# Mixture-of-experts stage of a two-block transformer: experts 0 and 1 placed ahead of the sort, 26 units of slots in place of 28

## The chip, the cores and the metric

One NeuronCore of a Trainium2 chip runs the whole program. The metric is the device time of one execution in microseconds (us); lower is better. The kernel before took 1778.32 us (median of 3 runs, 1778.24 to 1785.11).

## What is computed

A first transformer block (neighbourhood attention, grouped attention and a product-key expert layer) is followed by a second block (a gated-delta and an HGRN2 mixer, then a mixture of experts) and a last norm, on 256 tokens of width 1024 in fp32. The change lies in the mixture of experts alone:

```python
scores = sigmoid(xt @ w_router); sel = scores + router_bias
...
_, eidx = lax.top_k(where(emask, sel, -inf), TOP_K)      # 8 of 64 experts for each token
gates = ...                                              # normalised scores times 2.5
hg = einsum('td,edf->tef', x_b, w_gate)                  # every expert: 1024 -> 256, twice
hu = einsum('td,edf->tef', x_b, w_up)
routed = einsum('tef,efd->td', silu(hg) * hu * g, w_down)
shared = (silu(xt @ ws_gate) * (xt @ ws_up)) @ ws_down
```

With 256 tokens and 8 experts for each there are 2048 pairs of token and expert. The routing of the reference on these inputs leaves 14 experts with no token; the other 50 hold between 1 and 107.

## The kernel before

**Sort.** Once the router's scores are known, VectorE (DVE) picks each token's experts, counts the tokens of each expert, and ranks the 64 experts by falling count (`key`, `perm`). `lst` holds the expert of each rank as an address, `pos` and `V` hold for each token its place within the expert and its gate, both in the order of ranks. The counts and ranks are known only at the end of this chain; until then no weight of a routed expert can be addressed.

**Units.** The work on routed experts is cut into units of 128 slots (rows of TensorE's output). The 16 largest experts (`HEAVY`) have a unit of their own, ranks 16 to 29 share one in pairs of 64 slots, ranks 30 to 49 in fours of 32: 16 + 7 + 5 = 28 units, interleaved by a fractional key at the end of `moe`. If any expert has more tokens than its slots, or a rank past 49 has any, a branch at the end runs further units (`e.overflow`).

For each unit: `select` builds a 0/1 matrix S from `pos` (DVE), `tables` makes the slots' token numbers and gates from it (TensorE `pv`, DVE `sv` and `St`), `gather` multiplies the tokens by S, in 8 steps for a group of two units (TensorE `pga`, ScalarE `xg`), `gu_unit` multiplies by gate and up weights (`pgu`, 4 blocks of 128x1024 for each expert), `swiglu` and `turn` follow (`hh`, `phT`, `th`), `dn_block` multiplies by the down weights (`py`, 2 blocks for each expert), and `combine` adds the unit's rows back to the 256 tokens in two parts `yh` and `yl` (its output tiles show as `py` at L1771). An expert that has 64 or 32 slots uses 64 or 32 columns of the array: its matmul has that many stationary columns, and the experts of a unit lie side by side.

**Weights.** `wide_load` gives out buffers of 512 KB in a fixed ring (`load.raw`), and issues each load on the SP queue in program order. At this stage the ring has 25 places: 13 (11 of them `raw` tiles, 2 `mod` rows named `ada`), then 8 and 4 that held split weights (`whi`, `wlo`), which `load.raw.extend` adds just before `run`. A load waits until the last reader of its place is done. Before each load of a routed expert SP reads the expert's address from `lst` (`values_load`).

**Order.** The engines SP, PE, DVE and ACT run in the order in which the program is written (`m.manual`). In `run`, unit u goes through its four gate/up blocks, with steps of the next group's gather in between, then unit u - 2 is combined, then unit u - 1 goes through its down blocks. Two pieces of the shared expert (`shared_down`) stand within the sort.

Of the kernel before, what the change touches and what calls it, by code (L numbers as in the profile page):

```python
# [1393 lines left out]
HEAVY = 16  # L1394
MID = 30
LIGHT = 50
# [6 lines left out]
def wide_load(e, raw, parts):  # L1403
# [19 lines left out]
    return load  # L1423


def moe(e, a, x, m, late, out):
# [86 lines left out]
    def gu_unit(pg, xx, b, ws):  # L1513
        n = P // len(ws)
# [20 lines left out]
    def dn_block(py, th, k, w, last=True):  # L1535
        for q in range(2):
            for i in range(len(w)):
                t = slice(i * P // len(w), (i + 1) * P // len(w))
                nc.tensor.matmul(py[q][t], th[:, k, t], w[i][:, q * 512:(q + 1) * 512], start=k == 0, stop=last and k == 1)  # L1539
# [41 lines left out]
    wd = [load(a["ws_dn"][k], True) for k in range(2)]  # L1581
    hsh, psh = [], []

    def shared_down(tt, k):
        if k == 0:
            psh.append([ps.tile([P, 512], F32, tag="mm", name=uid(e, "py"), bufs=e.mm_bufs) for _ in range(2)])
        dn_block(psh[tt], hsh[tt], k, [wd[k]], last=False)
# [57 lines left out]
    nc.vector.scalar_tensor_tensor(num, pp[:, :2], 1.0, mk, op0=OP.add, op1=OP.mult)  # L1645
    idn = e.ident[:NE, :NE]
# [18 lines left out]
    more = pool.tile([1, 5], F32, name="more")  # L1665
    for k, (r, n) in enumerate(((0, 128.0), (HEAVY, 64.0), (MID, 32.0), (LIGHT, 0.0))):
        nc.vector.tensor_scalar(more[:, k:k + 1], pl[:, 1, r:r + 1], -n, 0.0, op0=OP.add, op1=OP.max)
    nc.vector.tensor_reduce(more[:, 4:5], more[:, 0:4], axis=AX.X, op=OP.max)
    moreu = pool.tile([1, 5], U32, name="moreu")
    nc.vector.tensor_copy(moreu, more)  # L1670
    pt = ps.tile([NE, 2, 2, P], F32, tag="tr", name="pT", bufs=e.tr_bufs)
# [3 lines left out]
    shared_down(1, 0)  # L1675
    tT = pool.tile([NE, 2, 2, P], F32, name="tT")
# [5 lines left out]
    shared_down(1, 1)  # L1682
    pos = pool.tile([P, 2, NE], F32, name="pos")
# [7 lines left out]
    def run(units, acc=()):  # L1691
# [10 lines left out]
        order = []  # L1702
        for u in range(len(units) + 1):
            for (which, n, v) in ((0, 4, u), (1, 2, u - 1)):
                if 0 <= v < len(units):
                    order += [(which, k, r) for k in range(n) for r in units[v][0]]
        ready = []
# [16 lines left out]
        def select(us):  # L1724

            S = wk.tile([P, 2, 2, P], F32R, tag="S", name=uid(e, "S"), bufs=2)
            for u, (ranks, base) in enumerate(us):
                r, n = ranks[0], len(ranks)
                nc.vector.tensor_tensor(S[:, :, u].rearrange("p t (r s) -> p t r s", r=n),
                                        io1[:, None, None, base:base + P // n].to_broadcast([P, 2, n, P // n]),  # L1730
                                        pos[:, :, r:r + n, None].to_broadcast([P, 2, n, P // n]), op=OP.is_equal)
            return us, S

        def tables(us, S):

            St = wk.tile([P, 2, T], F32R, tag="St", name=uid(e, "St"), bufs=4)
            sv = wk.tile([P, 2, 2], F32, tag="sv", name=uid(e, "sv"), bufs=3)
            pv = ps.tile([P, 2, 2], F32, tag="att", name=uid(e, "pv"), bufs=e.att_bufs)
            for u, (ranks, base) in enumerate(us):
                w = P // len(ranks)  # L1740
                for tt in range(2):
                    for i, r in enumerate(ranks):
                        t = slice(i * w, (i + 1) * w)
                        nc.tensor.matmul(pv[t, u], S[:, tt, u, t].bitcast(F32), V[:, tt, r], start=tt == 0, stop=tt == 1)
            n = len(us)
            nc.vector.tensor_copy(sv[:, :n], pv[:, :n])
            for u in range(n):
                nc.vector.tensor_scalar(St[:, u], iot, sv[:, u, 0:1], None, op0=OP.is_equal)
            xg = pool.tile([P, NC8, 2, P], F32, tag="xg", name=uid(e, "xg"), bufs=2)
            return S, St, [sv[:, u, 1:2] for u in range(n)], xg, us  # L1750

        def gather(g, q):

            S, xg, us = g[0], g[3], g[4]
            n = len(us)
            p = ps.tile([P, 2, P], F32, tag="att", name=uid(e, "pga"), bufs=e.att_bufs)
            steps = [(i, tt) for i in range(2) for tt in range(2)]
            for i, tt in steps:
                nc.tensor.matmul(p[:, :n].rearrange("p u n -> p (u n)"), hs[i][:, tt, q * P:(q + 1) * P],  # L1759
                                 S[:, tt, :n].rearrange("p u n -> p (u n)"), start=(i, tt) == steps[0],  # L1760
                                 stop=(i, tt) == steps[-1])
            nc.scalar.activation(xg[:, q, :n], p[:, :n], AF.Copy)  # L1762

# [10 lines left out]
        new, new2 = tables(*select(groups[0])), None  # L1774
        ahead(1)
        for q in range(2):
            gather(new, q)
        if len(groups) > 1:
            new2 = tables(*select(groups[1]))
# [3 lines left out]
        for u in range(len(units) + 1):  # L1783
            todo = []
            gi, i = divmod(u, 2)
            if u < len(units):
                if i == 0:
                    cur, new = new, new2
                if u == 0:
                    todo = [(cur, q) for q in range(2, 8)]  # L1790
                elif gi + 1 < len(groups):
                    todo = [(new, q) for q in range(4 if u > 1 else 0, 8)] if i else [(new, q) for q in range(4)]
                n, xx = len(units[u][0]), cur[3][:, :, i]
# [8 lines left out]
            for b in range(4):  # L1802
                if u < len(units):
                    gu_unit(pg, xx, b, weights(n))
                if b == 1 and h is not None:
                    th = turn(h)
                fetch(2 if u < 2 else FETCH[b])
# [13 lines left out]
            if done is not None:  # L1821
                py = down()
                n = len(units[u - 1][0])
                for k in range(2):
                    dn_block(py, th, k, weights(n))
# [31 lines left out]
    def shared_by(n, lo, hi, base):  # L1857
        return [(tuple(range(r, r + n)), base) for r in range(lo, hi, n)]


    kinds = [shared_by(1, 0, HEAVY, 0), shared_by(2, HEAVY, MID, 0), shared_by(4, MID, LIGHT, 0)]
    order = sorted(((j + (0.4, 0.6, 0.7)[k]) / len(us), u) for k, us in enumerate(kinds) for j, u in enumerate(us))
    units = [u for _, u in order]

    load.raw.extend([(early, 4, t) for _ in range(4) for t in ("whi", "wlo")])
# [112 lines left out]
```

## Time and profile before

| | |
|---|---|
| median of 3 runs | 1778.32 us (1778.24 to 1785.11) |
| the profiled execution | 1785.74 us, its span 1783.9 us |
| granted TensorE clock, mean over the span | 0.982 |
| busy: PE, DVE, ACT, POOL | 1687.5, 1133.2, 757.0, 192.8 us |
| the chain that ended last: PE, DVE, DMA | 68%, 17%, 7% of the span |
| bytes moved by DMA | 390.86 MB, mean 219 GB/s |
| weights of routed experts | 300 loads of 512 KB, issued from 1334.05 us on |

The span is the time from the first to the last instruction; what lies around it is 1.84 us here. In the 40 slices of the page each slice is 44.6 us; the mixture of experts takes the last ten. A matmul whose operands are fp32 appears twice in a view, as two records, so that one block of one expert's unit (two matmuls of 512 columns) is x4.

### The profile page before, as it was taken

The numbers are of one execution on the slowest core, as the hardware profiler recorded it, in microseconds if no ns is written. First come the engines' busy times: TensorE is split into PE (matmuls) and PEld (weight loads), VectorE is DVE, ScalarE is ACT, GpSimd is POOL, SyncE is SP. The second block draws the span as 40 slices with busy tenths as digits, with TensorE's granted clock in tenths as the row PEclk, the third lists the DMA queues.
The fourth block names the chain that finished last, engine by engine and source line by source line (L and its number), as shares of the span: only waits on it lengthen the run. The fifth ranks groups of instructions, "written<-read, shape, count | busy, mean of one in ns | idle before, by whom it ended". The sixth has DMA issues, their size and how long they took to land.

```text
span 1783.9 us, 28898 instructions
## 1 busy us (share of the span) xinstructions
PE 1687.5 (95%) x10939; PEld 1338.7 (75%) x10939; DVE 1133.2 (64%) x2209; ACT 757.0 (42%) x1240; POOL 192.8 (11%) x95
## 2 busy tenths in 40 slices
PE   6989998999999999999899998989989999999996
PEld 6778898999989999887678776978765554555543
DVE  5675789995979999777778676798571111111112
ACT  3557545344544444544444455655442222222222
POOL 1030001232112212000000003032020000000000
PEclk9999999999999999999999999999999999999998
DMA  6323654555435555688888754421129999999993
GB/s 232 128 83 118 210 161 152 159 173 189 154 125 163 172 170 166 200 285 292 280 282 285 246 182 149 159 95 48 76 91 409 409 395 362 375 364 340 410 356 122
DMA packets 108116, 390.86 MB, mean 219 GB/s; under 512 B 12657, under 2 KB 12945, under 8 KB 107841
## 3 DMA queue, kind: packets, MB, share of 16 engines
q1 hardware_dynamic: 106128, 384.58, 61.0%
q0 software_dynamic: 976, 2.82, 0.6%
q8 instruction: 88, 1.44, 0.3%
q10 hardware_dynamic: 864, 1.53, 0.3%
q14 instruction: 60, 0.48, 0.1%
HBM read 386.79 MB, written 2.10 MB: 218 GB/s over the span
## 4 chain that ended last, share of the span: by engine, by line
PE 68%; DVE 17%; DMA 7%; issue 4%; ACT 3%; POOL 0%; DVEq 0%; SPq 0%; ACTq 0%
PE pgu L1519 11%; PE acc L686 8%; DMA raw<-in_w_ada 6%; PE py L1539 6%; PE pu L80 5%; PE pu L82 5%; PE pu L81 5%; DVE wlo L67 5%; PE pga L1759 3%; PE py L1771 3%; PE pg L632 2%; ACT whi L66 2%; PE pmv L81 1%; PE pmv L82 1%; PE pmv L80 1%
## 5 line engine op out<-in xcount | busy, mean ns | idle before, releaser
L66 ACT ACTIVATE whi<-raw 128x1024 fp32r<-128x1024 f32 x366 | 384.5, 1054 | 306.3 <-PE pu L81 136.5
L67 DVE TENSOR_TENSOR wlo<-raw,whi 128x1024 fp32r<-128x1024 f32 x310 | 383.4, 1239 | 81.9 <-ACT whi L66 81.0
L82 PE MATMUL pu<-pxT,wlo 128*128 128x256 f32 x1024 | 289.6, 283 | 9.4 <-DVE wlo L67 6.7
L80 PE MATMUL pu<-pxT,whi 128*128 128x256 f32 x1024 | 292.1, 285 | 0.7 <-ACT whi L66 0.7
L81 PE MATMUL pu<-pxT,whi 128*128 128x256 f32 x1024 | 288.8, 282 | 0.0
L686 PE MATMUL acc<-whi,hh 128*128 128x512 f32 x1008 | 280.6, 396 | 7.7 <-ACT hh L66 4.6
L686 PEld LDWEIGHTS acc<-whi,hh 128*128 128x128 f32 x1008 | 188.8, 189 | 53.8 <-DVE hh L67 6.9
L67 POOL TENSOR_TENSOR wlo<-raw,whi 128x1024 fp32r<-128x1024 f32 x56 | 151.8, 2714 | 659.0 <-ACT whi L66 642.5
L82 PEld LDWEIGHTS pu<-pxT,wlo 128*128 128x128 f32 x1024 | 195.3, 191 | 11.5 <-DVE wlo L67 8.3
L1519 PE MATMUL pgu<-raw,xg 128*32 128x512 f32 (+2 forms) x720 | 203.4, 598 | 0.0
L80 PEld LDWEIGHTS pu<-pxT,whi 128*128 128x128 f32 x1024 | 195.3, 191 | 0.9 <-ACT whi L66 0.9
L81 PEld LDWEIGHTS pu<-pxT,whi 128*128 128x128 f32 x1024 | 195.3, 191 | 0.0
L686 PE MATMUL acc<-wlo,hh 128*128 128x512 f32 x504 | 157.8, 393 | 3.7 <-DVE wlo L67 3.7
L1519 PEld LDWEIGHTS pgu<-raw,xg 128*32 128x32 f32 (+2 forms) x720 | 66.8, 145 | 87.6 <-issue 81.0
L66 ACT ACTIVATE hh<-H 128x256 fp32r<-128x256 f32 x126 | 52.6, 417 | 176.8 <-PE acc L686 174.2
L686 PEld LDWEIGHTS acc<-wlo,hh 128*128 128x128 f32 x504 | 94.8, 189 | 25.7 <-DVE wlo L67 6.0
L67 DVE TENSOR_TENSOR yl<-py,yh 128x512 fp32r<-128x512 f32 x56 | 38.7, 692 | 117.7 <-ACT yh L66 117.7
L1539 PE MATMUL py<-raw,th 128*128 128x512 f32 (+2 forms) x400 | 109.3, 596 | 0.8 <-ACT th L1532 0.5
L1524 DVE SCALAR_TENSOR_TENSOR hh<-hh,sv,pgu 128x256 f32<-128x256 f32 x28 | 13.4, 478 | 138.1 <-ACT hh L1523 138.1
L1762 ACT ACTIVATE xg<-pga 128x256 f32<-128x256 f32 x112 | 43.1, 384 | 118.9 <-PE pga L1759 113.9
L771 DVE SCALAR_TENSOR_TENSOR ada<-raw,cs,ada 128x1024 f32<-128x1024 f32 x48 | 61.5, 1282 | 44.4 <-DMA raw<-in_w_ada 44.4
L66 ACT ACTIVATE yh<-py 128x512 fp32r<-128x512 f32 x56 | 33.5, 598 | 128.1 <-PE py L1539 128.1
(562 smaller groups left out, 2966.6 us busy)
## 6 DMA issues: line engine op xcount, KB each, us to landing
raw<-in_w_gu SPq DMA_DIRECT2D x180, 512.0 KB, 9.9
raw<-in_peer_u SPq DMA_DIRECT2D x128, 512.0 KB, 3.5
raw<-in_peer_v SPq DMA_DIRECT2D x128, 512.0 KB, 4.5
raw<-in_w_dn SPq DMA_DIRECT2D x96, 512.0 KB, 10.1
raw<-in_w_ada SPq DMA_DIRECT2D x48, 512.0 KB, 4.8
raw<-in_w_in_a SPq DMA_DIRECT2D x24, 512.0 KB, 3.6
ada<-in_w_gu SPq DMA_DIRECT2D x20, 512.0 KB, 9.2
raw<-in_w2a SPq DMA_DIRECT2D x17, 512.0 KB, 4.4
```

Of the source, the lines that this page charges most:

```text
L66: e.nc.scalar.activation(hi, src, AF.Copy)
L67: (eng or e.nc.vector).tensor_sub(lo, src, hi.bitcast(F32))
L80: nc.tensor.matmul(out, lh, rh, start=first, stop=False)
L81: nc.tensor.matmul(out, lh, rl, start=False, stop=False)
L82: nc.tensor.matmul(out, ll, rh, start=False, stop=last)
L686: nc.tensor.matmul(acc[tt][n], h[l][:, s], w[r][:, n * 512:(n + 1) * 512], start=j == order[0] and i == 0, stop=j == order[-1] and i == 2)
L771: nc.vector.scalar_tensor_tensor(mod[n], w, cs[:, c:c + 1], mod[n], op0=OP.mult, op1=OP.add)
L1519: nc.tensor.matmul(pg[t], xx[:, c, t], w[:, k * 512:(k + 1) * 512], start=c == 0, stop=c == NC8 - 1)
L1539: nc.tensor.matmul(py[q][t], th[:, k, t], w[i][:, q * 512:(q + 1) * 512], start=k == 0, stop=last and k == 1)
L1759: nc.tensor.matmul(p[:, :n].rearrange("p u n -> p (u n)"), hs[i][:, tt, q * P:(q + 1) * P], S[:, tt, :n].rearrange("p u n -> p (u n)"), st ...
L1762: nc.scalar.activation(xg[:, q, :n], p[:, :n], AF.Copy)
L1771: nc.tensor.matmul(acc[tt][n], St[:, tt * P:(tt + 1) * P], y[:, n * 512:(n + 1) * 512], start=first and v == 0 and w == 0, stop=v == len(u ...
```

## The change

It does three things.

1. Experts 0 and 1 (`STATIC`) get ranks 0 and 1 whatever they hold: `moe_cst` adds 2^17 and 2^16 to their keys. Their addresses are known from the start, so ten loads of their weights (`pre`) are issued ahead of the sort, straight after the shared expert's. Their S, tables and all 8 steps of their gather are made within the sort, from `num` and a small table `V0`, in place of `pos` and `V` (`first_group`). `select`, `tables` and `gather` move out of `run` for that, and `run` takes the finished group and the loads.
2. The slots are dealt anew: ranks 0 to 6 have 128, ranks 7 to 15 have 96 and share a unit with one expert of 32, ranks 16 to 29 have 64 in pairs, and the last 11 small experts fill three units: 2 + 5 + 9 + 7 + 3 = 26. `columns` cuts a unit of 96 + 32 slots into four tiles of 32 columns, three of which read the same weights.
3. The places of `whi` and `wlo` enter the ring at its head, behind the ten early loads.

```diff
+STATIC = 2
+WIDE = 7
+MID = 16
+LIGHT = 30
+REST = 50
...
+def columns(unit):
+    n = next(n for n in (P, 64, 32) if not any((hi - lo) % n for _, lo, hi, _ in unit))
+    return [(slice(t, t + n), i) for i, (_, lo, hi, _) in enumerate(unit) for t in range(lo, hi, n)]
+
+def mixture():
+    few = iter(range(LIGHT, REST))
+    kinds = [[shared((r, P)) for r in range(STATIC, WIDE)],
+             [shared((r, 96), (next(few), 32)) for r in range(WIDE, MID)],
+             [shared((r, 64), (r + 1, 64)) for r in range(MID, LIGHT, 2)]]
+    few = list(few)
+    kinds.append([shared(*((r, 32) for r in few[i:i + 4])) for i in (0, 4)] + [shared((few[8], 32), (few[9], 32), (few[10], 64))])
+    at = lambda k, j, n: j / (n - 1) if k == 0 else (j + 0.5) / n
...
-            for i, w in enumerate(ws):
-                t = slice(i * n, (i + 1) * n)
-                nc.tensor.matmul(pg[t], xx[:, c, t], w[:, k * 512:(k + 1) * 512], start=c == 0, stop=c == NC8 - 1)
+            for (t, i) in columns(unit):
+                nc.tensor.matmul(pg[t], xx[:, c, t], ws[i][:, k * 512:(k + 1) * 512], start=c == 0, stop=c == NC8 - 1)
...
     wd = [load(a["ws_dn"][k], True) for k in range(2)]
+    units = [[(r, 0, P, 0)] for r in range(STATIC)] + mixture()
+    sched = blocks_of(units)
+    pre = []
+    while sched[len(pre)][2] < STATIC:
+        which, b, r = sched[len(pre)]
+        pre.append(load((a["w_gu"], a["w_dn"])[which][(4, 2)[which] * r + b], True))
+
+    load.raw[:0] = [(early, 4, t) for _ in range(4) for t in ("whi", "wlo")]
+    load.raw[:0] = [(e.stage, e.w_bufs, t) for _ in range(e.w_bufs) for t in ("whi", "wlo")]
...
+    for tt in range(2):
+        nc.vector.tensor_copy(V0[:, tt, :, 0], cst[:, 1, tt:tt + 1].to_broadcast([P, STATIC]))
+        nc.vector.tensor_copy(V0[:, tt, :, 1], gate[:, tt, :STATIC])
+    first_group = tables(*select(units[:2]))
     pt = ps.tile([NE, 2, 2, P], F32, tag="tr", name="pT", bufs=e.tr_bufs)
...
     shared_down(1, 0)
+    for q in range(4):
+        gather(first_group, q)
...
     shared_down(1, 1)
+    for q in range(4, 8):
+        gather(first_group, q)
...
+                if late2 and u == 0 and b == 1:
+                    new = new2 = tables(*select(groups[1]))
...
-    load.raw.extend([(early, 4, t) for _ in range(4) for t in ("whi", "wlo")])
-    load.raw.extend([(e.stage, e.w_bufs, t) for _ in range(e.w_bufs) for t in ("whi", "wlo")])
-    run(units, psh)
+    run(units, psh, first_group, pre)
...
+    c[:, 1, 2:2 + STATIC] += 2.0 ** (17 - s[:STATIC])
```

**Where instructions move.** First TensorE within the sort, before: from the ranked list (`plist`) through the transposes of places and gates (`pT`) and the shared expert's down blocks (`py`) to the first table of a unit (`pv`).

```order
L1659 MATMUL plist<-perm,col 1x64
L1530 MATMUL phT_14421<-ident,hh_14418 128x128 x2
L1673 MATMUL pT<-ident,num 64x128
L1674 MATMUL pT<-ident,gate 64x128
L1673 MATMUL pT<-ident,num 64x128
L1674 MATMUL pT<-ident,gate 64x128
L1539 MATMUL py_14442<-raw_14325,th_14424 128x512
L1539 MATMUL py_14443<-raw_14325,th_14424 128x512
L1681 MATMUL pr<-perm,tT 128x64 x4
```

The same place in the change, from the transposes of the shared expert's hidden rows on (`L1760` and after are the new line numbers).

```order
L1570 MATMUL phT_14441<-ident,hh_14438 128x128 x2
L1728 MATMUL pv_14468<-V_14424,S_14463 128x2 x4
L1781 MATMUL pT<-ident,num 64x128
L1782 MATMUL pT<-ident,gate 64x128
L1781 MATMUL pT<-ident,num 64x128
L1782 MATMUL pT<-ident,gate 64x128
L1578 MATMUL py_14482<-raw_14325,th_14444 128x512
L1578 MATMUL py_14483<-raw_14325,th_14444 128x512
L1743 MATMUL pga_14486<-S_14463,hs_14166 128x256 x2
```

A table `pv` of the leading group now stands ahead of `pT`, and needs that group's S; the first gather steps stand ahead of `pr`.

Then the SP queue in the change, at the end of the ten early loads, which stand straight behind the shared expert's down weights: the last four of the ten, and the first read of `lst`. Before, the read of `lst` follows the shared expert's weights at once.

```order
L1417 DMA raw_14341<-in_w_gu 128x1024
L1417 DMA raw_14343<-in_w_gu 128x1024
L1417 DMA raw_14345<-in_w_dn 128x1024
L1417 DMA ada_9413<-in_w_dn 128x1024
L1811 TENSOR_LOAD lst
L1811 ISA x2
L1811 TENSOR_LOAD lst
```

These loads wait for no address, and fill ten of the 25 places of the ring; the last goes to a `mod` row.

Last, TensorE in the change where a unit of 128 slots ends its down blocks and the first unit of 96 + 32 slots begins its gate and up blocks.

```order
L1578 MATMUL py_14838<-raw_14645,th_14792 128x512
L1578 MATMUL py_14839<-raw_14645,th_14792 128x512
L1578 MATMUL py_14838<-raw_14647,th_14792 128x512
L1578 MATMUL py_14839<-raw_14647,th_14792 128x512
L1559 MATMUL pgu_14850<-raw_14669,xg_14596 32x512 x3
L1559 MATMUL pgu_14850<-raw_14714,xg_14596 32x512
```

Where the single expert has one matmul of 128 columns, the mixed unit has four tiles of 32: three on one expert's weights, one on the other's.

## Rows read from the trace of the kernel before

**Rows 1.** The page: busy tenths of 40 slices, PE and DMA.

```profile
PE   6989998999999999999899998989989999999996
DMA  6323654555435555688888754421129999999993
```

**Rows 2.** Stretches: us, busy PE, PEld, DVE, ACT, POOL (instructions), PEclk, DMA, GB/s.

```profile
1587.16:1617.25 30.09, 30.08 (x153) 15.72 (x152) 5.09 (x11) 6.78 (x16) 0.00 (x0) 1.00 1.03 409
1617.25:1647.99 30.74, 30.74 (x154) 15.54 (x152) 5.08 (x11) 6.79 (x16) 0.00 (x0) 1.00 0.85 314
...
1372.12:1723.98 351.86, 351.81 (x1751) 180.14 (x1749) 57.77 (x124) 78.00 (x184) 0.00 (x0) 1.00 0.97 377
```

**Rows 3.** Waits from 1345 us on: PE's for weights (total us, times, longest).

```profile
PEld pgu L1519 <- DMA raw<-in_w_dn: 1.3, 3, 0.8
PEld pgu L1519 <- DMA ada<-in_w_gu: 1.1, 2, 0.8
```

**Rows 4.** The chain that ended last, 1590 to 1650 us (start, us, what).

```profile
1594.75 3.57 PE py L1539 x32
...
1602.17 0.47 PE pga L1759 x4
1602.64 1.72 PE pgu L1519 x4
...
1610.30 3.43 PE py L1539 x8
1613.73 3.58 PE pgu L1519 x16
1617.32 0.37 PE phT L1530 x2
...
1618.15 1.87 PE pgu L1519 x8
...
1629.01 3.43 PE pgu L1519 x8
1632.44 0.22 PE phT L1530 x2
```

**Rows 5.** PE's timeline through the sort and into the first units, and its end.

```profile
1331.93 0.44 PE L1530 MATMUL phT<-ident,hh 128*128 128x128 f32 x2
1332.21 0.27 PE L1673 MATMUL pT<-ident,num 128*64 128x128 f32 x1
...
1337.61 0.83 PE L1744 MATMUL pv<-V,S 128*128 128x2 f32 x12
...
1349.32 3.85 PE L1519 MATMUL pgu<-raw,xg 128*128 128x512 f32 x12
...
1770.19 0.62 PE L1771 MATMUL py<-yl,St 128*128 128x512 f32 x2
```

**Rows 6.** DVE's timeline at the end of the sort.

```profile
1332.31 0.33 DVE L1667 TENSOR_SCALAR more<-plist 1x1 f32<-1x1 f32 x4
...
1332.86 0.16 DVE L1670 CAST moreu<-more 1x5 uint32<-1x5 f32 x1
...
1336.50 0.75 DVE L1729 TENSOR_TENSOR S<-io,pos 128x256 fp32r<-128x256 f32 x2
```

**Rows 7.** SP's timeline of loads around the sort.

```profile
1296.78 1.46 SPq L1413 DMA_DIRECT2D raw<-in_ws_dn  x2
1334.05 7.71 SPq L1413 DMA_DIRECT2D raw<-in_w_gu  x9
```

**Rows 8.** PE's timeline in the first block: two idle gaps, in brackets.

```profile
503.95 0.84 PE L632 MATMUL pg<-ow,oi 128*128 128x56 f16 x15 [1.84 <-DVE ow L628]
521.54 0.56 PE L632 MATMUL pg<-ow,oi 128*128 128x56 f16 x15 [1.86 <-DVE ow L628]
```

**Rows 9.** The granted clock (PEclk) in the stretches that follow these.

```profile
504.00:506.00 2.00, 2.00 (x21) 2.00 (x21) 1.97 (x5) 0.54 (x1) 0.00 (x0) 0.50 0.53 190
521.50:523.50 2.00, 1.96 (x28) 1.96 (x28) 2.00 (x5) 0.55 (x1) 0.00 (x0) 1.00 0.56 184
```

More of the change, by code (lines that the diff above doesn't have):

```diff
@@ L1423, in wide_load, with shared, blocks_of @@
     return load
+def shared(*ranks, base=0):
+    out, lo = [], 0
+    for r, n in ranks:
+        out.append((r, lo, lo + n, base))
+        lo += n
+    return out
+def columns(unit):
[9 more added lines that the diff above has]
+    at = lambda k, j, n: j / (n - 1) if k == 0 else (j + 0.5) / n
+    order = sorted((at(k, j, len(us)), k, u) for k, us in enumerate(kinds) for j, u in enumerate(us))
+    return [u for _, _, u in order]
+def blocks_of(units):
+    order = []
+    for u in range(len(units) + 1):
+        for (which, n, v) in ((0, 4, u), (1, 2, u - 1)):
+            if 0 <= v < len(units):
+                order += [(which, k, q[0]) for k in range(n) for q in units[v]]
+    return order
 def moe(e, a, x, m, late, out):
@@ L1533, in turn, with dn_block @@
         return th
[L1535 removed]
+    def dn_block(py, th, k, cols, w, last=True):
         for q in range(2):
[L1537 to L1538 removed]
+            for (t, i) in cols:
                 nc.tensor.matmul(py[q][t], th[:, k, t], w[i][:, q * 512:(q + 1) * 512], start=k == 0, stop=last and k == 1)
@@ new lines, in gather @@
+    def gather(g, q):
+        S, xg, us = g[0], g[3], g[4]
+        n = len(us)
+        p = ps.tile([P, 2, P], F32, tag="att", name=uid(e, "pga"), bufs=e.att_bufs)
+        steps = [(i, tt) for i in range(2) for tt in range(2)]
+        for i, tt in steps:
+            nc.tensor.matmul(p[:, :n].rearrange("p u n -> p (u n)"), hs[i][:, tt, q * P:(q + 1) * P],
+                             S[:, tt, :n].rearrange("p u n -> p (u n)"), start=(i, tt) == steps[0],
+                             stop=(i, tt) == steps[-1])
+        nc.scalar.activation(xg[:, q, :n], p[:, :n], AF.Copy)
@@ L1689, in moe, with run @@
         nc.vector.tensor_copy(V[:, tt, :, 0], cst[:, 1, tt:tt + 1].to_broadcast([P, NE]))
-    def run(units, acc=()):
+    place.update(pos=pos, V=V)
+    def run(units, acc=(), new=None, ready=()):
         groups = [units[i:i + 2] for i in range(0, len(units), 2)]
@@ L1700, in address @@
             return where[r]
[L1702 to L1707, printed above, removed]
+        order = blocks_of(units)
+        ready = list(ready)
         taken = [0]
@@ L1722, in weights @@
             return ready[taken[0] - n:taken[0]]
[L1724 to L1762, printed above, removed]
         def combine(v, St, yh, yl):
@@ L1772, in combine @@
                                          start=first and v == 0 and w == 0, stop=v == len(units) - 1 and w == 1)
-        new, new2 = tables(*select(groups[0])), None
+        new2 = None
         ahead(1)
-        for q in range(2):
-            gather(new, q)
-        if len(groups) > 1:
+        todo = []
+        if new is None:
+            new = tables(*select(groups[0]))
+            todo = [(new, q) for q in range(8)]
+            gather(*todo.pop(0))
+            gather(*todo.pop(0))
+        late2 = len(groups) > 1 and not todo
+        if len(groups) > 1 and todo:
             new2 = tables(*select(groups[1]))
@@ L1787, in run @@
                 if i == 0:
[L1788 to L1793, printed above, removed]
+                    cur, new, started = new, new2, False
+                if gi + 1 < len(groups) and (i or todo == []) and not (late2 and u == 0):
+                    todo = [(new, q) for q in range(0 if not started else 4, 8)] if i else [(new, q) for q in range(4)]
+                    started = not i
+                n, xx, fast = len(units[u]), cur[3][:, :, i], len(todo) > 4
                 pg = ps.tile([P, 512], F32, tag="tr", name=uid(e, "pgu"), bufs=e.tr_bufs)
@@ L1822, in run @@
                 py = down()
-                n = len(units[u - 1][0])
                 for k in range(2):
-                    dn_block(py, th, k, weights(n))
+                    dn_block(py, th, k, columns(units[u - 1]), weights(len(units[u - 1])))
                 yh = wk.tile([P, D], F32R, tag="yh", name=uid(e, "yh"), bufs=1)
```

77 lines of the change are left out of this document (53 added, 24 removed).

## The prediction

> **What bounds the kernel now.** I read the page's 40 slices first [rows 1]: in the last ten, the mixture of experts, PE stands at 9 and so does DMA. Two resources full at once leave open which one sets the pace, so the stretches came next [rows 2]. PE is busy for 351.81 of 351.86 us over 23 units, in stretches where DMA runs at its full 409 GB/s and just as much in stretches where it moves 314; a PE that waited for weights would show gaps in the first kind. The list of waits agrees: the two longest entries of PE waiting for a weight come to 2.4 us in 430 [rows 3]. So before the change **PE's own work** is the limit, and DMA has slack that it spends waiting for free places in the ring.
>
> A unit costs the same whether its 128 slots belong to one expert or to four. In the chain [rows 4] two blocks of gate and up weights take 3.43 us for one expert and 3.58 for two, and the down blocks 3.43 us for one and 3.57 for four: tiles of 32 or 64 columns run side by side. The small extra of a shared unit is 0.15 us for its first two blocks, 0.15 for each of the two later blocks, which stand apart between gather steps (1.87 against 1.72), 0.15 for the down blocks and 0.15 for the transposes behind them (0.37 against 0.22): 0.75 us. Two units between two such transposes take 30.09 us where parts of two shared units fall in, and 30.74 where more does [rows 2]. The 23 units hold 9 shared ones, so one of a single expert costs (351.86 - 9 x 0.75) / 23 = 15.0 us.
>
> **The change, part by part.**
>
> *26 units for 28.* Two units' work leaves PE: -2 x 15.0 = -30.0 us. The bytes stay: both deals serve 50 experts with 6 loads each. PE's cover for those loads is what shrinks.
>
> *More shared units.* Before 7 + 5 = 12, now 9 + 7 + 3 = 19: +7 x 0.75 = +5.2 us. A mixed unit runs four tiles of 32 columns, three on the same weights; no row shows tiles that share their weights, the nearest is four tiles on four weights (3.57 us for the down blocks), and I take that. Bounds for the whole term: +4.2 us, if the transposes' 0.15 isn't part of it, to the side by side failing, which is a rival below.
>
> Here a rule speaks against the change. The Trainium skill, "TensorE: Matmul & The Clock Gate", section "Measured speedup vs the span model", measured four packed tiles at 3.07 times, three at 2.38, so that four tiles would take 4 / 3.07 = 1.3 times as long as one. By that an estimate of a shared unit's 10.3 us in weights (3 x 3.43) would be 13.4, and seven more of them would give back 22 us. The trace of this kernel does not agree for four separate weights (3.57 against 3.43 is 1.04 times), and the measurement decides.
>
> *The lead.* The first group's S, tables and gather move from the head of `run` into the sort; by themselves they cost PE the same there. But PE has no holes to fill: from 1332.21 us it goes from one piece to the next up to the first units [rows 5]. What the move adds is a wait. `pv` of the leading group now stands ahead of `pT` on PE, and needs S, which DVE makes after `lst`, the overflow counts (one more reduction and one more subtraction, about 0.3 us) and four small copies into `V0` (about 0.4 us, at the price of the other small operations there). `moreu` is done at 1333.0 [rows 6], so these end at about 1333.7, and half of the two S (0.75 us together) makes the first one ready at 1334.1. PE is free at 1332.3, so it idles about 1.9 us, with `pT`, the shared expert's down blocks and everything else queued behind. Adding up the pieces from there (`pv` 0.7, `pT` 0.5, down blocks 1.9, four gather steps of 0.47 to 0.57, `pr` 1.0, down blocks 1.9, four steps, two blocks, a `pv` of 0.8, two blocks) unit 1 begins at about 1352.2. Before it begins after unit 0's last block, 1349.32 + 1.72 = 1351.0 [rows 4, 5]. The lead is **1.1 us worse**; bounds 0 (S ready in time) and +3.
>
> *The ten early loads.* Weights before were not late at the lead either, so early weights save PE nothing there. They are issued from about 1298 us [rows 7], when nothing else of size moves, and the reads of `lst` stay at 1334. Only two small POOL loads for the sort share the engines with them; the sort's uses of those lie over 10 us later. I price it at nothing, between 0 and +1.5.
>
> *Does DMA now bind?* A load takes 512 KB / 409 GB/s = 1.28 us. A shared unit of two experts needs 12 loads = 15.4 us against 15.75 on PE: even. A unit of four needs 30.8 and loses 15 us of lead, one of three loses 7, a single one gains 7. DMA's lead is capped by the ring's 25 places, 32 us, and the two leading units, whose weights but two are there, let it fill. In the order of the units the lead then goes 32, 17 behind the first unit of four, 31 after two single ones, 16 behind the second, 23, 16 behind the unit of three. Less about 7 us for places still being read, the closest approach is 9 us. DMA stays hidden, and without the early loads that margin would be gone.
>
> **The sum**: -30.0 + 5.2 + 1.1 = -23.7 us. Against the profiled execution, 1785.74 us, that is 1762.0. That execution lies 7.4 us above the median of the runs, 1778.32, whose slowest is 1785.11; a profile adds nothing that the change touches, so I apply the difference to the median: **1754.6 us**, -1.3%. A measurement of this kernel can tell about 0.5%, 9 us, from no change.
>
> **The rivals.**
>
> *The clock.* PE now idles some 1.9 us in the sort. Two idle gaps of nearly that length stand in the first block [rows 8]: after 1.84 us the granted clock was 0.50 in the next 2 us, 1.2 GHz, and after 1.86 us it was 1.00 [rows 9]. It can go either way here. A half clock over some 3 to 6 us costs 1.5 to 3 us: 1756 to 1758.
>
> *DMA becomes the bound.* For: the whole demand of 290 loads is 372 us, and PE will have about 395 us for it; over 23 units DMA averaged 377 GB/s [rows 2]. Against: that average includes idling for places, and full stretches hold 409. If a load took 1.40 us in the long run (374 GB/s), a unit of two would need 16.8 us, 1 us more than PE gives; over 19 shared units, less the lead, that is some 13 us: 1768.
>
> *Shared weights break the side by side* (the slower side). Three tiles of a mixed unit read one buffer at the same time. If tiles on one weight took turns, a step of 512 columns would take two turns or three instead of one: +0.43 us for each of 24 steps (10.3 us / 24), or +0.86. For nine mixed units +93 to +186 us: 1848 or more. It decides from 24 / 9 = 2.6 us for each mixed unit on; at about that price, a partial overlap, the time would be that of before, and below it the change still gains. Nothing in the trace shows a limit on reads, since four tiles on four buffers are fed at full pace.
>
> *The change does not do what it says*: an expert that outgrows its slots runs the branch for further units, at 15 us each and at least ten of them for ranks 7 to 15: over 1900. Counting the reference's routing gives 107, 103, 96, 89, 89 for ranks 2 to 6, 88 to 58 for ranks 7 to 15, 56 at rank 16, 31 at rank 30 and none at rank 50, so every rank fits.
>
> **How the numbers follow.** Forecast as summed 0.60; the clock 0.22; DMA bound 0.08; shared weights in turn or overlapping in part 0.04; overflow 0.02; and 0.04 for a gain lost in a way not listed. The forecast's own terms span 1752 (extra 4.2, lead 0) to 1758 (lead +3, early loads +1.5). Runs of one program lie up to 7 us apart here, so the low end takes in a little more gain, 1748, and the high end both a slower draw of the forecast (1762) and the DMA case, 1768. Faster by over 0.5% takes the forecast, the clock and most of the DMA case: 0.90. Within 0.5%: 0.04, from a partial overlap or a lost gain. Slower: 0.06.
>
> **What would show it.** Right: about 26 x 15.3 us of units with PE busy throughout and hardly a wait for weights; shared units at 15.7 us, mixed ones like pairs; an idle gap of PE near 1332 us that ends on DVE's S; ten loads issued between 1298 and 1320 us; PE's last matmul at about 1747 us in place of 1770.8 [rows 5]. Wrong: waits of PE on DMA in the units behind those of four experts, mixed units over 18 us, or an end of the last unit later than 1762.

## The result, and the profile after

The changed kernel took 1757.76 us (median of 4 runs, 1755.21 to 1763.74) beside 1781.71 us for the kernel before (now 4 runs, 1778.24 to 1787.91). The ratio is 0.9861, 95% interval 0.9840 to 0.9882: faster by 1.4%, 23.95 us between the medians. The forecast was a gain of 23.7 us to 1754.6, inside 1748 to 1768.

The page of the changed kernel, first. Each character is a 40th of its 1761.9 us.

```profile
PE   6989999899989999999999997987989999999996
DMA  6423654556545555587888754532067799999993
```

PE stands at 9 in the units as before [rows 1]. DMA shows the early loads in the slice from 1277 us, a 6 where a 2 stood, and is full from 1410 us on.

Over 22 units, from the transposes of one unit to those of another:

```profile
1374.76:1717.30 342.54, 342.34 (x2301) 155.16 (x2300) 55.09 (x124) 74.58 (x176) 0.00 (x0) 1.00 1.00 393
```

PE is busy for 342.34 of 342.54 us, and a unit takes 15.57 us on average, 15.30 before [rows 2]: 18 of the 22 are shared now, where 9 of 23 were. DMA moves 393 GB/s in place of 377, its share is 1.00, and still PE has no gaps. The list of PE's waits for weights from 1345 us on (total us, times, longest) grew, and stays small [rows 3]:

```profile
PEld pgu L1559 <- DMA raw<-in_w_gu: 3.0, 7, 0.8
PEld pgu L1559 <- DMA raw<-in_w_dn: 2.0, 5, 0.8
PEld pgu L1559 <- DMA ada<-in_w_dn: 0.8, 1, 0.8
PEld py L1578 <- DMA raw<-in_w_dn: 0.3, 1, 0.3
```

A weight load runs beside the matmul ahead of it, so most of these 6.1 us don't show as idle time of PE.

SP's queue around the sort. The ten early loads stand between 1301 and 1320 us; the first load that needs an address follows at 1336.15 [rows 7].

```profile
1301.06 8.88 SPq L1417 DMA_DIRECT2D raw<-in_w_gu  x8
1319.06 0.33 SPq L1417 DMA_DIRECT2D raw<-in_w_dn  x1
1319.51 0.35 SPq L1417 DMA_DIRECT2D ada<-in_w_dn  x1
1336.15 2.02 SPq L1417 DMA_DIRECT2D raw<-in_w_gu  x4
```

PE's timeline through the sort, and its last combine matmul [rows 5]:

```profile
1334.07 0.44 PE L1570 MATMUL phT<-ident,hh 128*128 128x128 f32 x2
1336.15 1.23 PE L1728 MATMUL pv<-V,S 128*128 128x2 f32 x8 [1.64 <-DVE S L1714]
1337.24 0.40 PE L1781 MATMUL pT<-ident,num 128*64 128x128 f32 x1
...
1338.07 2.96 PE L1578 MATMUL py<-raw,th 128*128 128x512 f32 x4
...
1748.20 0.63 PE L1840 MATMUL py<-yl,St 128*128 128x512 f32 x2
```

This is the wait that the change adds: PE idles 1.64 us ahead of `pv`, and DVE's S ends the wait. Behind it the same work takes longer than before: `pT` 0.40 to 0.42 us where it took 0.27 [rows 5], the shared expert's down blocks 2.96. Stretches of 2 us from the end of the wait (the column behind POOL is the granted clock) say why:

```profile
1336.15:1338.15 2.00, 2.00 (x13) 1.89 (x14) 0.89 (x4) 0.00 (x0) 0.00 (x0) 0.67 0.46 68
1338.15:1340.15 2.00, 2.00 (x4) 0.94 (x4) 0.76 (x2) 0.00 (x0) 0.00 (x0) 0.50 1.04 420
1340.15:1342.15 2.00, 1.98 (x11) 1.25 (x10) 0.00 (x0) 0.54 (x2) 0.00 (x0) 0.98 1.02 387
```

The clock falls to 0.50, 1.2 GHz, and is back at 2.4 GHz about 4 us behind the gap. The rival that I called the clock, with a chance of 0.22, happened beside the forecast: 33%, 50% and 2% of 2 us each, 1.7 us.

DVE at the end of the sort [rows 6]:

```profile
1334.70 0.33 DVE L1771 TENSOR_SCALAR more<-plist 1x1 f32<-1x1 f32 x4
...
1335.32 0.15 DVE L1776 COPY V<-ecst 128x2 f32<-128x2 f32 x1
...
1335.60 0.74 DVE L1714 TENSOR_TENSOR S<-io,num 128x256 fp32r<-128x256 f32 x2
```

S stands behind the overflow counts and the copies into `V0`, although `num`, all that it needs, is ready at 1332.2. The chain that ended last, in three places of the units [rows 4]:

```profile
1382.15 3.43 PE py L1578 x8
1385.59 3.57 PE pgu L1559 x32
...
1413.47 3.57 PE py L1578 x32
1417.04 3.43 PE pgu L1559 x32
1420.47 0.37 PE phT L1570 x2
1420.84 0.47 PE pga L1743 x4
1421.31 1.85 PE pgu L1559 x16
1423.17 0.67 PE pga L1743 x4
1423.83 1.85 PE pgu L1559 x16
1425.69 1.12 PE pga L1743 x8
...
1461.33 3.57 PE py L1578 x32
1464.89 3.63 PE pgu L1559 x8
```

A mixed unit's two blocks (x32, three of the four tiles on one buffer) take 3.57 us behind down blocks of another form (1385.59), and **3.43** (1417.04), no more than a single expert's, behind down blocks of the same four tiles. A single expert's two blocks (x8) take 3.63 behind four tiles. So the tiles themselves cost nothing; the change from one form to another does. That reading gets its own experiment below.

**What the runs are read by.** Runs of one kernel lie up to 17 us apart here, and much of that arises ahead of the change: in the profiled runs below, the shared expert's second `phT` starts anywhere from 1325.5 to 1334.1 us. From that `phT` to the start of the last combine matmul (`py<-yl`), the stretch that holds all that the change moves on PE, the profiles repeat: 414.13 us in the first profile and 414.13 in the second. I call it **the stretch**; behind it another 13.7 us follow in both kernels.

| kernel | from | to | the stretch, us | against before |
|---|---|---|---|---|
| before | 1331.93 | 1770.19 | 438.26 | |
| changed | 1334.07 | 1748.20 | 414.13 | -24.13 |
| changed, again | 1332.33 | 1746.46 | 414.13 | -24.13 |
| deal alone | 1325.85 | 1738.13 | 412.28 | -25.98 |
| lead alone | 1331.25 | 1769.97 | 438.72 | +0.46 |
| tables behind `pr` | 1329.69 | 1740.67 | 410.98 | -27.28 |
| the same, no early loads | 1325.53 | 1736.49 | 410.96 | -27.30 |
| the same, ring of 21 | 1326.24 | 1739.19 | 412.95 | -25.31 |
| the same, ring of 13 | 1332.06 | 1804.02 | 471.96 | +33.70 |
| the same, mixed as one tile | 1328.11 | 1733.85 | 405.74 | -32.52 |
| S early | 1326.58 | 1737.35 | 410.77 | -27.49 |
| S early, steps in pairs | 1332.09 | 1742.83 | 410.74 | -27.52 |
| S early, a step behind the combine | 1326.24 | 1732.07 | 405.83 | -32.43 |

### The profile page after: what moved, and what is told of

Same layout as the page of the kernel before. It is cut to its first block, busy times and chain, and to the rows that moved or that the text cites. A ratio compares the mean times of both kernels' runs of the same rounds, so it can differ in the third digit from the quotient of the medians.

```text
span 1761.9 us, 29814 instructions
## 1 busy us (share of the span) xinstructions
PE 1660.2 (94%) x11419; PEld 1307.8 (74%) x11419; DVE 1133.1 (64%) x2214; ACT 750.5 (43%) x1224; POOL 190.5 (11%) x95
## 4 chain that ended last, share of the span: by engine, by line
PE 67%; DVE 18%; DMA 7%; issue 4%; ACT 3%; POOL 0%; SPq 0%; DVEq 0%; ACTq 0%
PE pgu L1559 11%; PE acc L686 10%; PE py L1578 6%; PE pu L80 5%; PE pu L81 5%; PE pu L82 5%; DVE wlo L67 5%; DMA raw<-in_w_ada 4%; PE pga L1743 3%; PE py L1840 3%; PE pg L632 2%; ACT whi L66 2%; PE pmv L81 1%; PE pmv L82 1%; PE pmv L80 1%
## 5 line engine op out<-in xcount | busy, mean ns | idle before, releaser
L1559 PE MATMUL pgu<-raw,xg 128*32 128x512 f32 (+2 forms) x1012 | 193.8, 597 | 0.0
L1559 PEld LDWEIGHTS pgu<-raw,xg 128*32 128x32 f32 (+2 forms) x1012 | 55.6, 124 | 92.3 <-issue 82.1
L1578 PE MATMUL py<-raw,th 128*32 128x512 f32 (+2 forms) x504 | 99.9, 599 | 0.5 <-ACT th L1572 0.5
L1743 PEld LDWEIGHTS pga<-S,hs 128*128 128x128 f32 x416 | 54.5, 188 | 36.8 <-issue 36.1
```

What stands on the lines that cost most here:

```text
L1559: nc.tensor.matmul(pg[t], xx[:, c, t], ws[i][:, k * 512:(k + 1) * 512], start=c == 0, stop=c == NC8 - 1)
```

## Experiments

### The changed kernel again

No edit.

> The changed kernel as it is, run beside the next three on one chip. Both theories: 24 us below the kernel before (22 to 27), since nothing differs. It is the reference for the others: an idle gap of TensorE of 1.5 to 2 us ahead of the first table in the sort, and a granted clock of about 0.5 for some 3 us behind it in some profiles.

1759.75 us (1758.4 to 1765.1, 5 runs), ratio 0.9875 (0.9855 to 0.9895). The wait is 1.64 us again and the stretch the same to the hundredth.

### The deal alone

```diff
-    while sched[len(pre)][2] < STATIC:
...
-    first_group = tables(*select(units[:2]))
...
-    for q in range(4, 8):
-        gather(first_group, q)
...
-    run(units, psh, first_group, pre)
+    run(units, psh)
...
-    c[:, 1, 2:2 + STATIC] += 2.0 ** (17 - s[:STATIC])
```

> Only the new deal of slots, 26 units: all ranks by count, no early loads, no leading group in the sort, the gather of the first group back at the head of the units as before. Theory A (the whole gain is two units less of TensorE's work, and the ring of 25 buffers hides the loads without any head start): 25 to 27 us below the kernel before, 1 to 3 us below the changed kernel, waits of TensorE on weights under 5 us in all. Rival B (26 units need the head start of ten loads, or else the weights are late behind the units of four experts): 5 to 15 us slower than the changed kernel, with waits of TensorE on DMA in units 6 to 7 and 15 to 18.

1757.01 us, ratio 0.9864 (0.9844 to 0.9884); the stretch is 25.98 us shorter than before. So the deal is the whole gain, and more than the whole change gives. Weights don't come late without the early loads: PE's waits for them are 7.9 us in all beside 6.1, more than the 5 that theory A allowed, and none is over 0.8.

### The lead alone

```diff
-    kinds = [[shared((r, P)) for r in range(STATIC, WIDE)],
-             [shared((r, 96), (next(few), 32)) for r in range(WIDE, MID)],
+    kinds = [[shared((r, P)) for r in range(STATIC, MID)],
...
+             [shared(*((r + k, 32) for k in range(4))) for r in range(LIGHT, REST, 4)]]
```

> The lead alone: experts 0 and 1 first, their ten early loads and their gather in the sort, but the slots dealt as before, 28 units with 16 single ones, 7 pairs and 5 of four. Theory A (the lead saves TensorE nothing and adds a wait in the sort): 0 to 4 us slower than the kernel before. Rival B (weights and tokens fetched during the sort take work or waiting off the units): 4 to 12 us faster than the kernel before.

1784.21 us, ratio 0.9998 (0.9979 to 1.0018); the stretch is 0.46 us longer. The wait is there (1.64 us), the clock falls behind it, and the lead gains nothing.

### The tables of the leading group behind `pr`

```diff
-    first_group = tables(*select(units[:2]))
     pt = ps.tile([NE, 2, 2, P], F32, tag="tr", name="pT", bufs=e.tr_bufs)
...
-    for q in range(4):
-        gather(first_group, q)
     tT = pool.tile([NE, 2, 2, P], F32, name="tT")
...
             nc.tensor.matmul(pr[:, k, tt], tT[:, k, tt], perm, start=True, stop=True)
...
+    first_group = tables(*select(units[:2]))
+    for q in range(4):
+        gather(first_group, q)
```

> The leading group's table, its S and all eight gather steps are moved behind the sort's last transposes and the matmuls into pr; nothing else differs. Theory A (the wait of TensorE on S, and the fall of the clock behind it, are a loss of the change's own lead): no idle gap over 0.6 us in the sort, the clock stays at 1.0, and 1.6 us of wait plus up to 1.6 us of slow clock come back: 2 to 3.5 us below the changed kernel, 26 to 27 us below the kernel before. Rival B (the gap only moves to the next thing that is late, or the units absorb it): within 1 us of the changed kernel.

1757.83 us, ratio 0.9861 (0.9833 to 0.9888): the medians can't tell it from the changed kernel, the stretch can. It is 3.15 us shorter. PE goes from `phT` to `pT` without a gap, and the clock stays at 1.00. This version is the base of the next four.

### Without the early loads

```diff
-    while sched[len(pre)][2] < STATIC:
-        which, b, r = sched[len(pre)]
-        pre.append(load((a["w_gu"], a["w_dn"])[which][(4, 2)[which] * r + b], True))
```

> The later-tables version without the ten early loads; their weights are loaded like any others, once the sort has given the addresses. Read by the stretch from the shared expert's second phT to the last combine matmul, 410.98 us with them. Theory A (the early loads save PE nothing: the first weights are there in time either way, and the ring's places cap the lead): the same within 0.8 us, 410.2 to 411.8; waits of PE's weight loads on DMA a little longer at the lead and behind the first units of four, under 3 us more in all. Rival (the prediction's own sentence that without the early loads the margin would be gone, so that weights come late behind the units of three and four): 3 us or more longer, 414 or over, the new waits in those units. A gain of up to 0.5 us, should the loads disturb the sort, would show as 410.5.

1753.59 us, ratio 0.9821 (0.9796 to 0.9845); the stretch is 410.96 beside 410.98, and the waits for weights 7.1 us beside 5.6. The ten early loads save PE nothing, and cost it nothing.

### Fewer places in the ring

```diff
-    load.raw[:0] = [(early, 4, t) for _ in range(4) for t in ("whi", "wlo")]
-    load.raw[:0] = [(e.stage, e.w_bufs, t) for _ in range(e.w_bufs) for t in ("whi", "wlo")]
```

Both lines are left out for 13 places, the second alone for 21.

> The later-tables version with the 12 places of whi and wlo left out of the ring: 13 places in place of 25. Read by the stretch from the shared expert's second phT in the sort to the start of the last combine matmul, 410.98 us with 25 places. Theory A (DMA is hidden by the lead that the ring holds, so the lead is what the places are worth): walking the order of the units with 1.28 us for a load and 13 places, PE runs out of weights behind the units of three and four experts, about 14 us of waits in all (5 to 30), the stretch 416 to 441 us, and the waits stand in the list as PE's weight loads on DMA, most of them in the units just behind those of four. Rival (the lead is not needed; a shared unit of two is fed as it goes): under 3 us of new waits, the stretch within 3 us of 410.98. Rival (a DMA pace below 409 GB/s in the long run binds already at 25 places): the stretch grows by more than 30 us.

> The later-tables version with four places (whi and wlo of the stage) left out of the ring: 21 in place of 25. Read by the stretch from the shared expert's second phT to the last combine matmul: 410.98 us with 25 places, 471.96 with 13. Theory A (the lead that 25 places hold is more than the units of three and four experts use up): a walk of the units with 1.28 us for a load finds no wait at 21 places either, so the stretch stays within 1.5 us of 410.98 and the waits of PE's weight loads on DMA within 3 us of those at 25. Rival (13 places cost 61 us where the walk gave 14, so the walk overrates the lead and the margin at 25 is thin): 4 us or more longer at 21.

With 13 places 1821.41 us, ratio 1.0203 (1.0172 to 1.0235), the stretch 61 us longer. But this run does not test the theories. `ahead` keeps eight gate and up loads in front of the block at hand, and the down loads between them come on top: by the order in `run`, up to 20 loads are issued ahead of the block that reads them. With 13 places, 39 of the 300 loads go into a place whose block has not been issued yet. Such a block waits for what is loaded over its weights and reads that, which would also explain that part of this run's computation comes out changed. The longest waits are of this kind. SP's queue, and a block of a pair of experts on PE:

```profile
1441.60 1.60 SPq L1417 DMA_DIRECT2D ada<-in_w_gu  x2
...
1458.32 1.60 SPq L1417 DMA_DIRECT2D ada<-in_w_gu  x2
```

```profile
1468.58 4.92 PE L1559 MATMUL pgu<-ada,xg 128*64 128x512 f32 x8 [15.32 <-DMA ada<-in_w_gu]
```

The block's own weights are the two loads of 1441.60. The two of 1458.32 come 13 loads later, belong to the next unit and lie on the same two places, and PE waits for them. Three such waits (15.32, 8.08 and 15.44 us) are 38.8 of the 61 us; the rest I did not divide. So the 61 us, which the expectation for 21 places takes as a fact, are not the price of a short lead.

With 21 places no block is overtaken. The one run took 1754.65 us, and the stretch is 1.97 us longer, between what the two theories said. PE's two largest entries of waits for weights:

```profile
PEld pgu L1559 <- DMA raw<-in_w_gu: 4.9, 7, 1.8
PEld pgu L1559 <- DMA raw<-in_w_dn: 3.6, 7, 0.8
```

Almost all of the 1.97 us is lost in one place near the end: from the transposes during the last mixed unit to those during the last unit 15.01 us pass, 13.12 with 25 places. My walk of the units found no wait at 21 places, so the 9 us that the prediction gave as the closest approach is more than there is. That the lead in the ring is what hides DMA rests on this one run.

### Mixed units as one tile

```diff
 def columns(unit):
+    if unit[0][2] - unit[0][1] == 96:
+        return [(slice(0, P), 0)]
```

> The later-tables version, with each of the nine mixed units of 96 + 32 slots multiplied as one tile of 128 columns by the larger expert's weights; the products of the nine small experts with their own weights are left out, their loads stay. Read by the stretch from the shared expert's second phT to the last combine matmul, 410.98 us with the tiles. The forecast's term (0.75 us for each shared unit, tiles side by side whether they share weights or not): 9 x 0.75 = 6.8 us less, 404.2. The size read from the deal alone (0.57 each): 5.1 us less, 405.9. Rival (three tiles on one buffer take turns in part, 1.5 us or more a unit): 13.5 us less or more, under 397.5. Rival (units of one tile run faster than the weights come, so waits on DMA eat the gain): less than 3 us less, with longer waits of PE's weight loads on DMA.

One run, 1749.31 us. The stretch is 5.24 us shorter, 0.58 for each mixed unit: the size that the deal alone gave, and far from the rival's 13.5. In the chain a mixed unit now reads as a single one (blocks 1.72, steps 0.47 and 0.92, transposes 0.22). The units' matmuls save more than 5.24 us, though: the tables of such a unit get slower. Over the 12 tables in the chain `pv` takes 10.68 us where it took 8.42, since a group with tiles is cheaper there (0.64 us for 24 small matmuls) than two whole units (1.05 for 8). The rest, 5.24 + 2.26 = 7.5, is 0.83 for each unit, gather steps and transposes included.

### S made early

DVE's work for the leading group goes where its inputs are ready; PE's order stays that of the changed kernel.

```diff
     nc.vector.tensor_copy(mb, mk)
+    V0 = pool.tile([P, 2, STATIC, 2], F32, name="V0")
+    for tt in range(2):
+        nc.vector.tensor_copy(V0[:, tt, :, 0], cst[:, 1, tt:tt + 1].to_broadcast([P, STATIC]))
+        nc.vector.tensor_copy(V0[:, tt, :, 1], gate[:, tt, :STATIC])
...
     hsh.append(turn(swiglu(pg[1])))
+    first = select(units[:2])
...
-    first_group = tables(*select(units[:2]))
+    first_group = tables(*first)
```

> The changed kernel with DVE's work for the first group put where its inputs are ready: the four copies into V0 behind the copy mb, where DVE waits 0.84 us for ppos anyway, and the two S straight behind the shared expert's hh, ahead of lst and the overflow counts. PE's order stays, pv ahead of pT included. S's first half should then be ready at about the end of the transposes phT. Read by the stretch from the shared expert's second phT to the last combine matmul, 414.13 us in the changed kernel, 410.98 with the tables moved behind pr. Theory A (the lead's cost is the wait of 1.64 us and the low clock that follows it, nothing in the order of PE's pieces): the wait shrinks to 0.2 to 0.5 us, the granted clock stays at 1.00 in the stretch of 5 us behind it, and the stretch is 410.8 to 411.5. Rival B (the clock falls whatever the length of the gap): the wait shrinks but the clock is again 0.57 to 0.75 behind it, 412 to 413. Rival C (the order itself costs, pv and gather steps ahead of pT and pr): no wait, clock full, and still 413.5 or more.

1754.79 us, ratio 0.9849 (0.9824 to 0.9873); the stretch is 410.77, 3.36 us shorter than in the changed kernel. PE's timeline, and the two stretches of 5 us around it:

```profile
1326.58 0.44 PE L1570 MATMUL phT<-ident,hh 128*128 128x128 f32 x2
1326.97 1.02 PE L1731 MATMUL pv<-V,S 128*128 128x2 f32 x8
1327.86 0.28 PE L1782 MATMUL pT<-ident,num 128*64 128x128 f32 x1
```

```profile
1325.00:1330.00 5.00, 4.80 (x26) 2.73 (x24) 4.36 (x23) 0.38 (x1) 0.00 (x0) 1.00 0.00 0
1330.00:1335.00 5.00, 5.00 (x30) 3.74 (x28) 1.43 (x7) 1.54 (x4) 0.00 (x0) 1.00 0.92 333
```

No wait is left in front of `pv`, and the clock stays at 1.00. The stretch is just under theory A's range, which holds: what the lead costs is the wait and the low clock behind it, and the order of PE's pieces is no cost. Rival C falls. Rival B asked what a shorter gap does to the clock; no gap is left here, so this run does not test it.

### Gather steps in pairs

```diff
-FETCH = (0, 1, 1, 2)
+FETCH = (0, 2, 0, 2)
```

> The version with S made early (410.77 us from the shared expert's second phT to the last combine matmul), and the gather steps of a unit moved: two steps behind the second block and two behind the fourth, in place of one, one and two behind the second, third and fourth, so that no step stands between the third and the fourth block. Theory S (what a shared unit costs more is the change between tiles and whole-array matmuls, on each side, and not the tiles): in the changed kernel's chain a shared unit goes phT 0.37, step 0.47, block 1.85, step 0.67, block 1.85, two steps 1.12, in all 6.33 us; with the steps together phT 0.37, two steps 0.93, two blocks 3.57, two steps 1.12, in all 5.99. So 0.34 us less for each of the 18 shared units that have steps there, 6.1 us, the stretch 404.7 (404 to 405.5), and units of one expert unchanged. Rival T (the price belongs to the tiles or to their several weights): 410.8, the same within 0.5 us. Rival W (PE becomes so fast that weights come late, or the steps in pairs wait for their buffers): 406 to 410, with waits of PE on DMA or on ACT's xg that were not there.

1757.33 us, ratio 0.9830 (0.9806 to 0.9854), and a stretch of 410.74: no gain. By the time alone rival T would have won. The chain of one unit and a row of the waits tell another story:

```profile
1384.16 0.37 PE phT L1570 x2
1384.53 0.47 PE pga L1746 x4
...
1385.00 0.73 PE pga L1746 x4
1385.74 3.57 PE pgu L1559 x32
1389.31 1.14 PE pga L1746 x8
```

```profile
PEld pga L1746 <- ACT th L1572: 4.8, 23, 0.3
```

The third and fourth block take 3.57 us together where they took 1.85 twice, so the change of form saved what theory S said. The second step of the pair took 0.73 in place of 0.47, 23 times, waiting for ACT: the saving went into a new wait.

### A step behind the combine

```diff
-FETCH = (0, 1, 1, 2)
+FETCH = (0, 1, 0, 2)
...
                 combine(u - 2, *y)
                 y = None
+            fetch()
```

> The version with S made early (410.77 us from the shared expert's second phT to the last combine matmul), with a unit's gather steps at other places: one behind the second block, none behind the third, two behind the fourth, one behind the combine. No step stands between the third and fourth block, and no two stand straight behind the transposes, where the second of a pair took 0.73 us and waited for ACT's th. The step behind the combine has whole-array matmuls ahead of it and the down blocks behind it, so it adds no change between tiles and whole array. Theory S (the price of a shared unit is the change between tiles and whole-array matmuls; the version with steps in pairs saved it in the blocks and gave it back in the wait for th): a shared unit's blocks stand together at 3.57 us, its single steps take 0.47, and 0.33 us are left out in each of 18 units: 6 us less, 404.8 (404.2 to 405.5). Rival T (no gain is to be had there; the two blocks' 3.57 in the version before came with an equal loss that will show elsewhere): 410.2 to 411. Rival W (the new step waits for a buffer or holds up the down blocks, or weights come late): 406 to 410, with that wait in the list.

1749.10 us (1745.8 to 1758.04, 6 runs), ratio 0.9818 (0.9793 to 0.9843); the stretch is 405.83, 4.94 us shorter than with S early and 8.3 shorter than in the changed kernel. The chain through one mixed unit, and where a microsecond of the expected 6 stayed:

```profile
1377.98 0.37 PE phT L1570 x2
1378.35 0.47 PE pga L1746 x4
1378.82 3.57 PE pgu L1559 x32
1382.39 1.14 PE pga L1746 x8
...
1386.23 0.47 PE pga L1746 x4
...
1700.43 4.49 PE pgu L1559 x32
```

Every step takes 0.47 and the blocks stand together. From the transposes of one unit to those of the next, each of the 18 shared units takes 0.32 to 0.35 us less than before the move, 6 us as expected. At the end 1.1 us are lost again: the last mixed unit's two blocks at 1700.43 took 4.49 us in place of 3.57, and the weight loads there waited for DMA, since PE now runs that much earlier. It is the place where the ring of 21 lost its 2 us. Theory S holds, with a little of rival W. By the stretch and by the ratio this is the fastest of the versions that leave nothing out.

## Why the prediction was right

**Two units less, seven more shared.** The forecast had -30.0 + 5.2 = -24.8 us; the deal alone gives -25.98, 1.2 us more. At 15.0 us for a unit, the seven shared ones cost 4.0 us in place of 5.2, 0.57 each where I took 0.75. That is the net of three things which I left out. The tables are cheaper for units with tiles, by some 2.2 us: `pv` takes 12.6 us of the chain in the stretch before and 9.4 in the deal alone, where one table in 14 less would save 0.9. The gather steps of a shared unit are dearer, by 0.4 us for each, 2.8 for seven: 0.67 for a step between two blocks, where a single unit's take 0.47 [rows 4], and 1.15 for the two steps behind the fourth block in place of 0.93. And shared units now often follow each other, which saves some 1.5 us: 4 single units take 3.63 us for their first two blocks where 7 did, and 6 units of four tiles take 3.43, which none did before. Together 5.2 - 2.2 + 2.8 - 1.5 = 4.3 us, close to the 4.0. These are rows of the kernel before: a single unit's two blocks and its last two steps, then the steps of a pair:

```profile
1598.32 3.63 PE pgu L1519 x8
...
1606.55 0.93 PE pga L1759 x8
...
1620.02 0.67 PE pga L1759 x4
...
1622.56 1.15 PE pga L1759 x8
```

The experiment with mixed units as one tile shows the first two together: 0.83 for the tiles, steps included, less 0.25 in the tables. I also read the 0.15 of a block as a price of tiles. It is the price of changing form between a matmul on all 128 columns and one on 64 or 32, and it was to be seen ahead of the change: the 3.63 us at 1598.32 are a single expert's two blocks behind the four tiles of `py` at 1594.75, beside 3.43 behind its own form [rows 4].

**Tiles that share their weights** run side by side: 3.43 us for a mixed unit's two blocks. The estimate of 1.3 times as long, worked out from the Trainium skill, "TensorE: Matmul & The Clock Gate", section "Measured speedup vs the span model", does not come true here: the runs show 1.00 to 1.04 times, and they decide. What the runs do agree with is the Trainium skill, "TensorEngine Tiling (Array Packing)", section "Key Properties", by which a change of the tiling mode drains TensorE: 0.13 to 0.20 us are lost at each change of form. That a drain is what takes this time, no run here shows.

**The lead.** Net it cost 1.85 us (the changed kernel against the deal alone) where I had 1.1, by parts that I had otherwise. The wait on S was 1.64 us for a forecast 1.9, in the place and on the engine named. The clock was put apart as a rival and came with it: wait and clock together are 3.36 us, shown by making S early. And without them the lead is 1.51 us better than the order before (410.77 against 412.28), where my sum of the pieces made it 0.8 better. The parts do not add up everywhere: on the old deal the same lead costs 0.46 us, not 1.85. Of the 1.4 us between them, 0.4 lie ahead of the first unit's transposes (+1.94 us on the old deal, +2.34 on the new). The other 1.0 lies behind them, where the version with the lead alone also has its units in another order than before, a single one second where a pair stood. So this comparison does not price the lead by itself, and the 1.4 us stay open.

**DMA.** It stayed hidden, as forecast, and PE's own work is still the limit. One sentence was wrong: that without the early loads the margin would be gone. Leaving them out changes the stretch by 0.02 us. The lead of the DMA is set by the ring's places, whatever it holds at the start; taking 4 of the 25 away costs 2 us, in one run. So the margin was thinner than my walk made it, and lay in the ring and not in the early loads. In the last version, 8.3 us faster in the stretch, it is used up.

**The sum.** -25.98 + 1.85 = -24.13 us in the stretch, for a forecast of -23.7. That they agree to 0.4 us is in part luck: the units saved 1.2 us more than forecast, the lead cost 0.75 us more, and the two errors offset each other. The median of 1757.76 lies 3.2 us above the forecast, and the kernel before has moved as much: with a fourth run its median is 1781.71, 3.4 above that of the first three. The difference of the medians is 23.95 us.

## What to carry to other kernels

An experiment's time can stay the same while its mechanism works: the steps in pairs saved what was expected and gave it to a new wait, and only the chain and the list of waits told the two apart, which led to the version 8.3 us faster in the stretch. A run that leaves out too much can test something else: a ring has to have as many places as the program loads ahead, 20 here, or the blocks read the wrong weights. Where runs spread by more than the effect, find a stretch between two fixed instructions that repeats, and read the edits there. When work is moved ahead on one engine, move what it waits for as well: PE's `pv` went forward, DVE's S stayed behind small work that nobody waited for, and a gap of 1.64 us cost twice its length, since the clock fell behind it.

## What the runs showed of the hardware

After the idle gap of 1.64 us PE's granted clock fell to 0.50, 1.2 GHz, and was back at 2.4 GHz 4 to 5 us behind the gap, in all three profiles that have it; gaps of 0.47 and 0.20 us in the same part of the other versions left it at 1.00. In the first block a gap of 1.84 us lowered it and one of 1.86 did not [rows 8, 9], so the length of a gap alone doesn't decide. Tiles of 32 and of 64 columns count as two forms: two blocks of 64-column tiles behind 32-column ones take 3.58 us.
